# S5's pre-norm applied after its input matmuls, and 256 more transfers issued by GpSimd

## The chip, the cores and the metric

The kernel runs on one core of one Trainium2 chip. The metric is the device time of one execution in microseconds (us): before the change the median of three runs is 2486.29 us (2485.32 to 2488.64). One further execution was taken by the hardware profiler; its own time is 2485.38 us. Engines are named PE (TensorE), DVE (VectorE), ACT (ScalarE), POOL (GpSimd) and SP (SyncE, here only an issuer of DMA transfers); PEld is PE's weight load.

## The reference

A sequence of 512 tokens of 1024 channels goes through two blocks of two layers each, in fp32: a pooling mixer and a gated convolution FFN (ffn0), sliding-window attention and a second such FFN (ffn1); then an S5 mixer and an MLP, an SSD mixer and an MLP. The second block is modulated by a condition vector `c`. What the change touches is this part:

```python
cond = silu(c)
mod = cond @ ada_w[i] + ada_b[i]                  # 1024 x 6144, i = 0, 1
sh1, sc1, g1, sh2, sc2, g2 = split(mod, 6)
h = rmsnorm(x, norm_mix_g[i]) * (1 + sc1) + sh1   # layer 0 of block two: S5
u = h @ s5_w_in
y = s5_recurrence(u, lambda, log_dt, b, c) + d * u
x = x + g1 * (val * sigmoid(gate)),  val, gate = split(gelu(y) @ w_glu + b_glu)
```

## The kernel before

Activations are kept transposed: eight tiles `xT[k]` of 128 channels by 512 tokens. A matrix product in fp32 is made from three matmuls of rounded parts (`mm3`, L218 to L220: high by high, high by low, low by high). A weight chunk `ws` of up to 512 KB is fetched by SP (L190), split by ACT into `wh` (L203) and by DVE into `wl` (L204); three `ws` buffers rotate. Each engine runs a fixed list of instructions in order, and the DMA issues of SP, ACT and POOL stand in such a list too: an issue that waits for a buffer holds what stands behind it in that list.

A layer ends in halves of 256 tokens: its output matmuls (`tail`), the sum of squares `acc` (L294, L295), `Norm.rs` (L303 on PE, L305 on ACT, L306 and L309 on DVE, L312 on PE), which leaves the reciprocal rms on all partitions in PSUM, and then `post_add`, which adds the normed output to `xT` (L434 and L437 on DVE). `post_add` can carry the next layer's pre-norm in its stages. There are two classes of pre-norm. `PreNorm` (L363) waits for the next `Norm.rs`, makes `u = x*gs*rs` (L388), and splits `u + shift` into two parts (L391 on ACT, L392 on DVE) that the matmuls read. `PreScale` (L404) splits `x*gain` inside `post_add` (L418, L419), before the rms is known, and the rms multiplies the matmuls' result. Before the change `PreScale` serves attention and the two FFNs, and `PreNorm` serves S5, SSD and the MLPs.

The modulation (`ada_units`) is a product of a vector and a matrix, made by `vecmat`: twelve blocks of 512 columns, each of eight steps. A step fetches 256 KB as `as` (L483, two buffers) and adds it, scaled, to `aa` on DVE (L486 first, L488 then). At a block's end `aa` is split into three parts by turns of ACT (L496) and DVE (L498), and PE sums over the partitions into a PSUM tile `pn` (L472) that DVE reduces (L475). `aa` has one buffer, and `pn` has one buffer that `vecmat` shares with `Norm.rs`. Generators of such background work are advanced while a layer's matmuls run: S5's tables and matrices beside ffn0 (`d_tab`, `d_k`, `bs`, `cs`, `dd` in the rows), the first modulation and S5's Toeplitz blocks (`tz`, `th`) beside ffn1, the second modulation beside the first MLP. What is left is drained before the next layer.

In S5, `u_out` takes the result of the input matmuls from PSUM with an ACT copy into `usc`, ACT sends it to HBM (`d_u`), and SP fetches it rearranged as `U`. The tables come back from HBM as `vt` (POOL), `rot` and `ct` (SP).

At the start POOL builds four pooling masks (`band`, L830 to L837) that DVE completes (L851) and PE uses (L882).

Of the kernel before, what the change touches and what calls it, by code (L numbers as in the profile page):

```python
# [11 lines left out]
F32 = mybir.dt.float32  # L12
# [9 lines left out]
P = 128  # L22
# [40 lines left out]
def net_kernel(ctx: ExitStack, tc: tile.TileContext, I: dict, out: bass.AP, parts=ALL):  # L63
# [21 lines left out]
    def tt(s="t", dt=F32):  # L85
        return tp.tile([P, S], dt, tag="t", name=nm(s))
# [14 lines left out]
    V.memset(ones, 1.0)  # L101
    one16 = cst.tile([P, 1], BF16, name="one16")
    V.memset(one16, 1.0)
    eps1 = cst.tile([P, 1], F32, name="eps1")
    V.memset(eps1, 1e-6)
    eps2 = cst.tile([P, 1], F32, name="eps2")
    V.memset(eps2, 1e-5)
    mod = cst.tile([P, 96], F32, name="mod")
    cond = cst.tile([P, KD], F32, name="cond")
    cond_set = []  # L110
    recent = {}

# [127 lines left out]
    class Held:  # L240
# [3 lines left out]
        def __init__(self, runs):  # L244
            self.runs, self.ch, self.ap = runs, {}, {}
# [109 lines left out]
    def behind(instructions):  # L355

        with ExitStack() as stack:
            for ins in instructions:
                stack.enter_context(tc.issue_after(ins))
            yield  # L360

    class PreNorm:

        late = False

        def __init__(self, norm, eps, modulate):
            self.norm, self.eps, self.modulate = norm, eps, modulate
            self.h = None
            i, m, gname = modulate
            self.gs = cst.tile([P, KD], F32, tag="gs", bufs=2, name=nm("gs"))  # L370
            c = i * 48 + (m + 1) * 8
            go = voff[gname] + 8 * i
            V.scalar_tensor_tensor(self.gs, mod[:, c:c + 8], 1.0, vec[:, go:go + 8], ALU.add, ALU.mult)

        def parts(self, span):
            return ()
# [27 lines left out]
    class PreScale(PreNorm):  # L404

        late = True

        def __init__(self, norm, eps, gain=None):
            self.norm, self.eps, self.gain = norm, eps, gain
            self.h = [(ht(), ht()) for _ in range(KD)]  # L410
            self.rs = None

        def parts(self, span):

            ts = slice(*span)
            g = [1.0 if self.gain is None else vc(self.gain[0], self.gain[1] + k) for k in range(KD)]
            hi, lo = ([h[i][:, ts] for h in self.h] for i in range(2))
            return (lambda k: A.activation(hi[k], xT[k][:, ts], AF.Copy, scale=g[k]),  # L418
                    lambda k: V.scalar_tensor_tensor(lo[k], xT[k][:, ts], g[k], f(hi[k]), ALU.mult, ALU.subtract))  # L419
# [43 lines left out]

    def vecmat(pool, W, ncb, col, done):

        def total(parts, cb):
            ps = psn.tile([P, 512], F32, tag="n", name=nm("pn"))
            for j in range(3):  # L470
                for q in range(4):
                    T.matmul(ps[:, 4 * q + j:4 * q + j + 1], parts[j][:, q * P:(q + 1) * P], one16,  # L472
                             start=True, stop=True)
            sums = cst.tile([P, 4], F32, tag="asum", bufs=2, name=nm("sums"))
            V.tensor_reduce(sums, ps[:, :16].rearrange("p (q j) -> p q j", q=4)[:, :, :3], AX.X, ALU.add)  # L475
            done(cb, sums)

        due = None
        for cb in range(ncb):
            acc = None  # L480
            for k in range(KD):
                st = pool.tile([P, 512], F32, tag="as", bufs=2, name=nm("as"))
                nc.sync.dma_start(st, W[k * P:(k + 1) * P, cb * 512:(cb + 1) * 512])  # L483
                if k == 0:
                    acc = pool.tile([P, 512], F32, tag="aa", bufs=1, name=nm("aa"))
                    V.tensor_scalar(acc, st, col(k), None, ALU.mult)  # L486
                else:
                    V.scalar_tensor_tensor(acc, st, col(k), acc, ALU.mult, ALU.add)  # L488
                if k % 2:
                    yield  # L490
                if k == 1 and due is not None:
                    total(*due)
            t2 = tt("ab").bitcast(BF16)
            parts = [t2[:, :512], t2[:, 512:], pool.tile([P, 512], BF16, tag="ab", bufs=1, name=nm("ab"))]
            for j in range(3):
                A.activation(parts[j], acc, AF.Copy)  # L496
                if j < 2:
                    V.tensor_tensor(acc, acc, parts[j], ALU.subtract)  # L498
            due = parts, cb
        yield  # L500
        total(*due)

    def ada_units(pool, i):

        if not cond_set:
            cond_set.append(True)
            c0 = voff["c_2"]
            with behind([recent["split"]]):
                A.activation(cond, vec[:, c0:c0 + KD], AF.Silu)
            yield  # L510

        def done(cb, sums):
            c = i * 48 + cb * 4
            bo = voff["ada_b_2"] + c
            V.tensor_tensor(mod[:, c:c + 4], sums, vec[:, bo:bo + 4], ALU.add)

        yield from vecmat(pool, I["ada_w_2"][i], 12, lambda k: cond[:, k:k + 1], done)

    def s5_tables(pool, dr):

# [132 lines left out]
    def s5_phasors(dr, n, far, near):  # L653

        g8 = slice(8 * n, 8 * n + 8)
        wide = lambda t: t.rearrange("p (g a b) -> p g a b", g=8, a=8)
        fr, fi = (t[:, g8].unsqueeze(3).broadcast_to([P, 8, 8, 8]) for t in far)
        nr_, ni_ = (t[:, g8].unsqueeze(2).broadcast_to([P, 8, 8, 8]) for t in near)
        for i, (a, b, c, d, op) in enumerate(((fr, nr_, fi, ni_, ALU.subtract), (fr, ni_, fi, nr_, ALU.add))):
            o, t = tt("ph"), tt("ph")  # L660
            V.tensor_tensor(wide(o), a, b, ALU.mult)
            V.tensor_tensor(wide(t), c, d, ALU.mult)
            V.tensor_tensor(o, o, t, op)
            nc.sync.dma_start(dr["tab"][n][:, 512 * i:512 * i + 512], o)
            yield

    def s5_mats(pool, dr, pr, pi, vr, vi, cr, ci, sg):
        zt = tt("s5z")[:, :P]
        V.memset(zt, 0.0)
        for gb in range(8):  # L670
            nc.sync.dma_start(dr["k"][8 * gb:8 * gb + 8, :, 0].rearrange("g h j -> (g h) j"), zt)
        dg = pool.tile([16, 64], F32, name="s5dg")
        with nc.allow_non_contiguous_dma("4 KB"):
            nc.sync.dma_start(dg, I["s5_d_2"][0].rearrange("(g h) -> h g", h=16))
# [3 lines left out]
        def load(gb):  # L678
            g8 = slice(8 * gb, 8 * gb + 8)
            bs = pool.tile([P, 2, 8, 16], F32, tag="bs", bufs=1, name=nm("bs"))  # L680
            for e, (u, v) in enumerate(((bre, bim), (bim, bre))):
                nc.sync.dma_start(bs[:64, e], u[g8].rearrange("g p h -> p g h"))
                nc.sync.dma_start(bs[64:, e], v[g8].rearrange("g p h -> p g h"))
            cs = pool.tile([P, 2, 2, 64], F32, tag="cs", bufs=1, name=nm("cs"))
            for e, (u, v) in enumerate(((cre, cim), (cim, cre))):
                nc.sync.dma_start(cs[:, e, 0], u[g8].rearrange("g h p -> (g h) p"))
                nc.sync.dma_start(cs[:, e, 1], v[g8].rearrange("g h p -> (g h) p"))
            return bs, cs

        nxt = load(0)  # L690
# [74 lines left out]
    def s5_toeplitz(pool, dr):  # L765

        for n in range(8):
            g8 = slice(8 * n, 8 * n + 8)
            tz = pool.tile([P, 8, P], F32, tag="tz", bufs=2, name=nm("tz"))
            for s in range(8):  # L770
                j = (8 - s) * 16
                nc.sync.dma_start(tz[16 * s:16 * s + 16], dr["kflat"][g8, :, j:j + P].rearrange("g h j -> h g j"))
            yield
            th = pool.tile([P, 8, P], F32, tag="th", bufs=1, name=nm("th"))
            A.activation(th.rearrange("p g (h t) -> p g t h", h=16), tz.rearrange("p g (t h) -> p g t h", t=8), AF.Copy)  # L775
            nc.scalar.dma_start(dr["tab"][n][:, 3072:], th.rearrange("p g j -> p (g j)"))
            yield
# [532 lines left out]
    def s5_layer(dr, pool, pa):  # L1310
# [15 lines left out]
        def ctabs(n):  # L1326
            if n < KD:
                ct[n] = pool.tile([P, 2, 8, P], F32, tag="ct", bufs=2, name=nm("ct"))
                nc.sync.dma_start(ct[n].rearrange("p i g j -> p (i g j)"), dr["tab"][n][:, 2048:])

        def u_out(n, ps, span=FULL):
            if span[0] == 0:
                U[n] = tt("usc")
            usc = U[n]
            cs = slice(span[0] // 8, span[1] // 8)
            a = A.activation(usc.rearrange("p (s c) -> p s c", s=8)[:, :, cs], ps.rearrange("p (c s) -> p s c", s=8),
                             AF.Copy)
# [137 lines left out]
        def tail_(hf, nxt):  # L1475
# [23 lines left out]
            for q in range(2):  # L1499
                glu(6 + q, pp[0][:, 256 * q:256 * q + 256], pp[1][:, 256 * q:256 * q + 256], HALVES[hf])  # L1500

        return Layer(lambda nxt: PreNorm(nxt, eps2, (0, 0, "norm_mix_g_2")), load, head, body_, tail_,
                     lambda span, nxt, pre: None)


# [424 lines left out]
        bgps[0] = psmm  # L1930

    rope_c = {}
    s5_on = "s5" in names
    ada_on = [any(p in names for p in q) for q in (("s5", "mlp0"), ("ssd", "mlp1"))]
    ada_due = [i for i in range(2) if ada_on[i]]
    tables_due, toeplitz_due = s5_on, s5_on
# [103 lines left out]
```

## Time and profile before

| | |
|---|---|
| median of three runs | 2486.29 us (2485.32 to 2488.64) |
| the profiled execution | 2485.38 us, of which the span of its instructions is 2483.7 us |
| PE busy | 2340.7 us, 94% of the span |
| DVE, ACT, POOL busy | 69%, 46%, 14% |
| mean granted PE clock | 0.972 of 2.4 GHz |
| DMA | 311 MB, 125 GB/s on average; SP's queue 278 MB, POOL's 13.6 MB |

The places that the text speaks of, in us from the span's start: the pooling layer up to about 30, ffn0 to 480, attention to 735, ffn1 to 1114 (its tail from 1084), S5's input to about 1180, S5 to 1330.

In the rows, `idle before` in square brackets is how long the engine stood before the instruction, and what released it. The views by window give busy time and number of instructions of each engine, the granted clock and the DMA engines' share. A row of the DMA view ends with the median time from issue to landing.

### The profile page before, as it was taken

What the parts mean: (1) busy time and instruction counts of PE and PEld (TensorE: products, weight loads), DVE (VectorE), ACT (ScalarE), POOL (GpSimd) and SP (SyncE); (2) the same over time, 40 slices, a digit from 0 to 9 for tenths busy, and PEclk for the clock granted to TensorE, in tenths of its full rate; (3) what the DMA queues carried; (4) which work ended last, traced back from release to release, by engine and by line L of the source; (5) the groups of instructions that cost most, each with busy time, mean ns of one, the idle gap of its engine ahead of it and who ended that gap; (6) DMA issues with size and microseconds to landing.
All of it is one profiled execution on the core that took longest, in us unless ns stands there. A gap on an engine that the chain in (4) does not pass through costs nothing.

```text
span 2483.7 us, 33557 instructions
## 1 busy us (share of the span) xinstructions
PE 2340.7 (94%) x12397; PEld 1972.1 (79%) x12397; DVE 1713.8 (69%) x3069; ACT 1142.1 (46%) x2038; POOL 337.9 (14%) x345
## 2 busy tenths in 40 slices
PE   7999999788979999986899999999999999999998
PEld 7877777776778888875878887889878888888888
DVE  6896989678658778786655666666777788633333
ACT  6543535467665444344543433334555554422332
POOL 1001223201200000000110210110143331200110
PEclk9999999889989999997999999999999999999999
DMA  4224443311274555552942455543433332232222
GB/s 122 88 88 140 131 142 103 125 52 51 75 206 134 180 178 165 179 173 68 306 153 77 143 166 191 188 134 92 125 105 99 107 104 80 93 102 94 95 88 72
DMA packets 297780, 311.29 MB, mean 125 GB/s; under 512 B 53569, under 2 KB 251025, under 8 KB 296593
## 3 DMA queue, kind: packets, MB, share of 16 engines
q1 hardware_dynamic: 270033, 278.22, 36.0%
q10 hardware_dynamic: 23680, 17.31, 2.3%
q0 software_dynamic: 3904, 13.63, 1.7%
q8 instruction: 97, 1.59, 0.3%
q14 instruction: 66, 0.54, 0.1%
HBM read 284.92 MB, written 24.18 MB: 124 GB/s over the span
## 4 chain that ended last, share of the span: by engine, by line
PE 74%; DVE 12%; DMA 6%; ACT 4%; issue 3%; SPq 0%; POOL 0%; DVEq 0%; ACTq 0%; POOLq 0%
PE mm L219 22%; PE mm L218 22%; PE mm L220 22%; DMA as<-in_ada_w 3%; DVE wl L204 3%; ACT wh L203 1%; DVE aa L488 1%; PE mm L1642 1%; PE mm L1643 1%; PE mm L1644 1%; PE pb L1712 1%; PE pb L754 1%; DMA tz<-d_k 1%; ACT th L775 1%; DMA d_u<-usc 1%
## 5 line engine op out<-in xcount | busy, mean ns | idle before, releaser
L218 PE MATMUL mm<-h,wh 128*128 128x512 f32 (+1 forms) x1792 | 665.6, 374 | 22.9 <-ACT h L418 7.2
L219 PE MATMUL mm<-h,wh 128*128 128x512 f32 (+1 forms) x1792 | 666.1, 372 | 6.2 <-DVE h L392 3.3
L220 PE MATMUL mm<-h,wl 128*128 128x512 f32 (+1 forms) x1792 | 664.8, 372 | 1.7 <-DVE wl L204 1.7
L203 ACT ACTIVATE wh<-ws 128x1024 fp32r<-128x1024 f32 (+1 forms) x367 | 388.0, 1060 | 563.3 <-PE mm L219 479.6
L204 DVE TENSOR_TENSOR wl<-ws,wh 128x1024 fp32r<-128x1024 f32 (+1 forms) x367 | 466.0, 1272 | 240.7 <-ACT wh L203 234.3
L218 PEld LDWEIGHTS mm<-h,wh 128*128 128x128 f32 x1792 | 346.8, 194 | 81.0 <-issue 8.5
L219 PEld LDWEIGHTS mm<-h,wh 128*128 128x128 f32 x1792 | 347.1, 194 | 63.3 <-DVE h L392 5.4
L220 PEld LDWEIGHTS mm<-h,wl 128*128 128x128 f32 x1792 | 347.3, 194 | 56.3 <-DVE wl L204 2.5
L218 PE MATMUL mm<-hi,wh 128*128 128x512 f32 (+1 forms) x1056 | 369.5, 354 | 9.0 <-ACT wh L203 7.6
L219 PE MATMUL mm<-lo,wh 128*128 128x512 f32 (+1 forms) x1056 | 372.0, 353 | 1.7 <-DVE lo L319 1.7
L220 PE MATMUL mm<-hi,wl 128*128 128x512 f32 (+1 forms) x1056 | 370.8, 353 | 0.8 <-DVE wl L204 0.8
L218 PEld LDWEIGHTS mm<-hi,wh 128*128 128x128 f32 x1056 | 200.6, 190 | 37.3 <-ACT wh L203 8.7
L219 PEld LDWEIGHTS mm<-lo,wh 128*128 128x128 f32 x1056 | 201.4, 191 | 28.5 <-DVE lo L319 2.7
L220 PEld LDWEIGHTS mm<-hi,wl 128*128 128x128 f32 x1056 | 201.2, 191 | 26.8 <-DVE wl L204 1.0
L488 DVE SCALAR_TENSOR_TENSOR aa<-as,cond,aa 128x512 f32<-128x512 f32 x168 | 132.0, 786 | 113.8 <-DMA as<-in_ada_w 112.3
L1266 POOL TENSOR_TENSOR r<-r 128x512 f32<-128x512 f32 x64 | 88.1, 1379 | 671.1 <-ACT r L1262 488.0
L760 POOL TENSOR_TENSOR dd<-ident,s5dg 16x64 f32<-16x64 f32 x16 | 69.4, 4337 | 343.1 <-DVE kt L762 336.1
L319 DVE TENSOR_TENSOR lo<-r,hi 128x512 fp32r<-128x512 f32 x64 | 48.1, 756 | 76.5 <-ACT hi L317 76.4
L1287 DVE SCALAR_TENSOR_TENSOR x<-mm,mod,x 128x512 f32<-128x512 f32 (+1 forms) x76 | 48.9, 662 | 60.6 <-PE mm L220 60.4
L496 ACT ACTIVATE ab<-aa 128x512 bf16<-128x512 f32 x72 | 44.9, 624 | 97.0 <-DVE aa L488 61.7
L317 ACT ACTIVATE hi<-r 128x512 fp32r<-128x512 f32 x64 | 40.4, 631 | 72.3 <-POOL r L1266 72.3
L295 DVE TENSOR_TENSOR acc<-acc,sq 128x256 f32<-128x256 f32 (+1 forms) x148 | 62.0, 432 | 16.4 <-ACT sq L294 11.6
(484 smaller groups left out, 3651.2 us busy)
## 6 DMA issues: line engine op xcount, KB each, us to landing
ws<-in_mlp_w SPq DMA_DIRECT2D x124, 512.0 KB, 4.0
as<-in_ada_w SPq DMA_DIRECT2D x192, 256.0 KB, 3.1
ws<-in_ffn_w_in SPq DMA_DIRECT2D x88, 512.0 KB, 3.8
ws<-in_m_w_in SPq DMA_DIRECT2D x41, 512.0 KB, 3.7
ws<-in_ffn_w_out SPq DMA_DIRECT2D x40, 512.0 KB, 3.5
ws<-in_w_o SPq DMA_DIRECT2D x16, 512.0 KB, 3.4
ct<-d_tab SPq DMA_DIRECT2D x8, 1024.0 KB, 9.5
ws<-in_s_w_glu SPq DMA_DIRECT2D x16, 512.0 KB, 5.8
```

The costliest lines, as they stand in the source:

```text
L203: A.activation(h_, s_, AF.Copy)
L204: V.tensor_tensor(l_, s_, f(h_), ALU.subtract)
L218: T.matmul(ps, wh, xh, start=first, stop=False)
L219: T.matmul(ps, wh, xl, start=False, stop=False)
L220: return T.matmul(ps, wl, xh, start=False, stop=last).ins
L295: V.tensor_tensor(dst, dst, sq[:, a:b], ALU.add)
L319: return hi_, V.tensor_tensor(lo[:, ts], src, f(hi[:, ts]), ALU.subtract)
L488: V.scalar_tensor_tensor(acc, st, col(k), acc, ALU.mult, ALU.add)
L496: A.activation(parts[j], acc, AF.Copy)
L760: G.tensor_tensor(dd, ident[:16, :16].unsqueeze(1).broadcast_to([16, 4, 16]), dg[:, g4].unsqueeze(2).broadcast_to([16, 4, 16]), ALU.mult)
L1266: G.tensor_tensor(r, r, r, ALU.mult)
L1287: V.scalar_tensor_tensor(xT[n][:, ts], ps, md(i, 5, n), xT[n][:, ts], ALU.mult, ALU.add)
```

## The change

S5's pre-norm becomes a `PreScale` with the modulation's gain. The reciprocal rms then multiplies the result of S5's input matmuls in `u_out` (one more DVE instruction on each evacuation), and the shift goes through the matmuls by itself: `s5c = shift @ s5_w_in`, made by two further blocks of `vecmat` behind the first modulation's twelve (16 transfers of 256 KB and 16 DVE steps), and added as ACT's bias.

Besides, these transfers are issued by POOL and no longer by SP: the first modulation's 96 `as` (with the 16 new ones 112), 16 `d_tab<-ph`, 8 `d_k<-s5z`, 32 `bs`, 32 `cs`, 64 `tz` and 8 `ct`. The second modulation stays with SP. The two epsilons move into one tile. Line numbers of the changed kernel are higher by 20 in most places: `as` is issued at L495, steps are L498 and L500, splits L514, the reduce L487, `post_add` L445 and L448.

```diff
     class PreScale:
-        def __init__(self, norm, eps, gain=None):
+        def __init__(self, norm, eps, gain=None, modulate=None):
+            self.norm, self.eps = norm, eps
+            if modulate is not None:
+                gs = modulated(*modulate)
+                self.gain = lambda k: gs[:, k:k + 1]
...
-    def vecmat(pool, W, ncb, col, done):
+    def vecmat(pool, W, ncb, col, done, perm=False, queue=nc.gpsimd):
...
-                nc.sync.dma_start(st, W[k * P:(k + 1) * P, cb * 512:(cb + 1) * 512])
+                queue.dma_start(st, W[k * P:(k + 1) * P, cb * 512:(cb + 1) * 512])
...
-        yield from vecmat(pool, I["ada_w_2"][i], 12, lambda k: cond[:, k:k + 1], done)
+        yield from vecmat(pool, I["ada_w_2"][i], 12, lambda k: cond[:, k:k + 1], done,
+                          queue=nc.sync if i else nc.gpsimd)
+        if i == 0 and s5_on:
+            yield from vecmat(pool, I["s5_w_in_2"][0], 2, lambda k: md(0, 0, k),
+                              lambda cb, sums: V.tensor_copy(s5c[:, 4 * cb:4 * cb + 4], sums), perm=True)
...
-                nc.sync.dma_start(bs[:64, e], u[g8].rearrange("g p h -> p g h"))
+                nc.gpsimd.dma_start(bs[:64, e], u[g8].rearrange("g p h -> p g h"))
...
-                nc.sync.dma_start(ct[n].rearrange("p i g j -> p (i g j)"), dr["tab"][n][:, 2048:])
+                nc.gpsimd.dma_start(ct[n].rearrange("p i g j -> p (i g j)"), dr["tab"][n][:, 2048:])
...
-            a = A.activation(usc.rearrange("p (s c) -> p s c", s=8)[:, :, cs], ps.rearrange("p (c s) -> p s c", s=8),
-                             AF.Copy)
+            t = tt("us")[:, :span[1] - span[0]]
+            V.tensor_tensor(t, ps, S_["pre"].rs[:, slice(*span)], ALU.mult)
+            a = A.activation(usc.rearrange("p (s c) -> p s c", s=8)[:, :, cs], t.rearrange("p (c s) -> p s c", s=8),
+                             AF.Identity, bias=s5c[:, n:n + 1])
...
-        return Layer(lambda nxt: PreNorm(nxt, eps2, (0, 0, "norm_mix_g_2")), load, head, body_, tail_,
+        return Layer(lambda nxt: PreScale(nxt, eps2, modulate=(0, 0, "norm_mix_g_2")), load, head, body_, tail_,
```

The instructions that the rows below name stand in this order on their engines. First DVE at the seam from ffn1 to S5, from the last step of the modulation's twelfth block to the first addition of `post_add` in the kernel before (`f<-f,mm` are ffn1's last sums, `acc` the post-norm's):

```order
L488 SCALAR_TENSOR_TENSOR aa_10079<-as_10115,cond,aa_10079 128x512
L498 TENSOR_TENSOR aa_10079<-aa_10079,ab_10118 128x512
...
L498 TENSOR_TENSOR aa_10079<-aa_10079,ab_10118 128x512
...
L475 TENSOR_REDUCE sums_10138<-pn_10125 128x4
...
L306 RECIPROCAL sr_10359<-sr_10359 128x2
L309 TENSOR_SCALAR dg_10362<-ident,sr_10359 128x128 x2
L979 TENSOR_TENSOR f_8330<-f_8330,mm_10606 128x256
L979 TENSOR_TENSOR f_8346<-f_8346,mm_10606 128x256
L204 TENSOR_TENSOR wl_10771<-ws_10769,wh_10770 128x1024
L434 SCALAR_TENSOR_TENSOR u_10367<-f_8045,vec,pn_10356 128x256
```

The same place of DVE in the changed kernel, from ffn1's last sums to the first addition of `post_add`; `aa_10143` and `aa_10175` are the two blocks of the shift's product, and the twelfth block, with the first steps of `aa_10143`, stands ahead of the piece:

```order
L999 TENSOR_TENSOR f_8346<-f_8346,mm_10675 128x256
...
L500 SCALAR_TENSOR_TENSOR aa_10143<-as_10157,mod,aa_10143 128x512
...
L514 TENSOR_TENSOR aa_10143<-aa_10143,ab_10166 128x4x16x8 x2
L498 TENSOR_SCALAR aa_10175<-as_10173,mod 128x512
...
L500 SCALAR_TENSOR_TENSOR aa_10175<-as_10211,mod,aa_10175 128x512
L514 TENSOR_TENSOR aa_10175<-aa_10175,ab_10214 128x4x16x8
...
L514 TENSOR_TENSOR aa_10175<-aa_10175,ab_10214 128x4x16x8
...
L487 TENSOR_REDUCE sums_10234<-pn_10221 128x4
L537 COPY s5c<-sums_10234 128x4
L308 RECIPROCAL sr_10471<-sr_10471 128x2
L311 TENSOR_SCALAR dg_10474<-ident,sr_10471 128x128 x2
L445 SCALAR_TENSOR_TENSOR u_10479<-f_8045,vec,pn_10468 128x256
```

The last three steps of one block, the whole of another, their splits and their sums now stand between ffn1's last sum and the post-norm's reciprocal.

Second, POOL at the start of the program, before (`band` are the pooling masks, `dd` a product with S5's vector `d`):

```order
L830 AFFINE_SELECT band_164<-band_164 128x128 x2
L832 MEMSET band_178 128x384
L830 AFFINE_SELECT band_178<-band_178 128x128 x3
L837 MEMSET band_178 128x1 x15
L830 AFFINE_SELECT band_178<-band_178 128x128 x2
L760 TENSOR_TENSOR dd_2191<-ident,s5dg 16x64
```

And in the changed kernel, where eight transfers (`bs`, `cs`) stand ahead of the first mask's last parts:

```order
L850 AFFINE_SELECT band_146<-band_146 128x128
L703 DMA bs_1830<-in_s_b_re 64x8x16
L706 DMA cs_1835<-in_s_c_re 128x64
...
L857 MEMSET band_164 128x1 x7
L780 TENSOR_TENSOR dd_2191<-ident,s5dg 16x64
L850 AFFINE_SELECT band_164<-band_164 128x128 x2
L852 MEMSET band_178 128x384
L850 AFFINE_SELECT band_178<-band_178 128x128 x3
L857 MEMSET band_178 128x1 x15
L850 AFFINE_SELECT band_178<-band_178 128x128 x2
```

The product `dd`, which reads the loaded vector `s5dg`, has moved ahead of the last part of the third mask and the whole of the fourth.

## Rows read from the trace of the kernel before

**Rows 1.** The page, busy time of PE and its share.
```profile
PE 2340.7 (94%) x12397; PEld 1972.1 (79%) x12397; DVE 1713.8 (69%) x3069; ACT 1142.1 (46%) x2038; POOL 337.9 (14%) x345
```

**Rows 2.** Windows: us, busy (count) per engine, PEclk, DMA share, GB/s.
```profile
800.00:1050.00 250.00, 249.85 (x1195) 202.22 (x1194) 193.75 (x280) 104.42 (x138) 1.27 (x2) 1.00 0.54 174
...
1120.00:1150.00 30.00, 16.87 (x112) 16.01 (x112) 20.73 (x57) 10.67 (x28) 0.00 (x0) 0.73 0.13 44
```

**Rows 3.** Timeline of PE, the seam: start, us, instruction, idle before.
```profile
1126.67 1.19 PE L303 MATMUL pn<-ones,acc 128*128 128x128 f32 x4 [11.91 <-DVE acc L295]
...
1131.13 0.79 PE L218 MATMUL mm<-h,wh 128*128 128x256 f32 x2 [1.11 <-ACT h L391]
```

**Rows 4.** S5's input sent to HBM: count, ns min/median/max, first and last start.
```profile
L1341 ACTq DMA_DIRECT2D d_u<-usc x8: 366/373/540, 1173.7 to 1199.1; - x8
```

**Rows 5.** Timeline of DVE at the seam.
```profile
1085.63 0.49 DVE L486 TENSOR_SCALAR aa<-as,cond 128x512 f32<-128x512 f32 x1 [1.34 <-ACT ab L496]
...
1096.17 0.75 DVE L488 SCALAR_TENSOR_TENSOR aa<-as,cond,aa 128x512 f32<-128x512 f32 x1 [1.02 <-DMA as<-in_ada_w]
...
1097.62 0.75 DVE L488 SCALAR_TENSOR_TENSOR aa<-as,cond,aa 128x512 f32<-128x512 f32 x1
...
1109.20 0.15 DVE L475 TENSOR_REDUCE sums<-pn 128x4 f32<-128x12 f32 x1
...
1117.31 0.86 DVE L434 SCALAR_TENSOR_TENSOR u<-f,vec,pn 128x256 f32<-128x256 f32 x2
```

**Rows 6.** Timeline of ACT at the seam.
```profile
1098.40 0.63 ACT L496 ACTIVATE ab<-aa 128x512 bf16<-128x512 f32 x1 [12.80 <-DVE aa L488]
...
1104.13 0.62 ACT L496 ACTIVATE ab<-aa 128x512 bf16<-128x512 f32 x1
...
1110.26 0.24 ACT L305 ACTIVATE sr<-pn,eps 128x2 f32<-128x2 f32 x1
```

**Rows 7.** Issue of `as` by SP, ns min/median/max, 740 to 1120.
```profile
L483 SPq DMA_DIRECT2D as<-in_ada_w x94: 327/328/458, 771.9 to 1094.5; - x94
```

**Rows 8.** Issue of `vt` by POOL, the same columns.
```profile
L1321 POOL DMA_DIRECT2D vt<-d_tab x16: 536/536/722, 1002.4 to 1228.1; - x16
```

**Rows 9.** DMA view, 960 to 1060: count, KB, median us to landing.
```profile
as<-in_ada_w SPq DMA_DIRECT2D x33, 256.0 KB, 3.4
...
vt<-d_tab POOLq DMA_DIRECT2D x2, 256.0 KB, 5.2
```

**Rows 10.** DMA view, 1080 to 1120.
```profile
as<-in_ada_w SPq DMA_DIRECT2D x6, 256.0 KB, 2.7
vt<-d_tab POOLq DMA_DIRECT2D x6, 256.0 KB, 6.9
```

**Rows 11.** Timeline of PE at the seam from ffn0 to attention.
```profile
489.00 1.19 PE L312 MATMUL pn<-dg,ones 128*128 128x128 f32 x4 [0.97 <-DVE dg L309]
```

**Rows 12.** Windows, the end of that seam.
```profile
525.00:530.00 5.00, 2.37 (x19) 2.01 (x17) 4.38 (x13) 4.62 (x12) 0.00 (x0) 1.00 0.79 256
```

**Rows 13.** Waits of DVE, 740 to 1120: us, times, longest.
```profile
DVE aa L488 <- DMA as<-in_ada_w: 46.9, 39, 3.0
```

**Rows 14.** Timeline of POOL at the start.
```profile
10.77 0.78 POOL L830 TENSOR_SCALAR_AFFINE_SELECT band<-band 128x128 f32<-128x128 f32 x2
18.42 0.28 POOL L760 TENSOR_TENSOR dd<-ident,s5dg 16x64 f32<-16x64 f32 x1 [6.88 <-DMA s5dg<-in_s_d]
```

**Rows 15.** Timeline of DVE at the start.
```profile
13.94 1.28 DVE L851 TENSOR_TENSOR band<-band,ident 128x128 f32<-128x128 f32 x6
```

**Rows 16.** The page, `dd`: busy, mean ns, idle before.
```profile
L760 POOL TENSOR_TENSOR dd<-ident,s5dg 16x64 f32<-16x64 f32 x16 | 69.4, 4337 | 343.1 <-DVE kt L762 336.1
```

**Rows 17.** Waits of PE, 30 to 480.
```profile
PE mm L218 <- ACT wh L203: 6.1, 3, 3.2
PE mm L218 <- DVE u L939: 6.1, 1, 6.1
```

**Rows 18.** Waits of PE, 640 to 760.
```profile
PE pn L312 <- DVE dg L309: 7.0, 2, 6.1
```

More of the change, by code (lines that the diff above doesn't have):

```diff
@@ L103, in net_kernel @@
     V.memset(one16, 1.0)
-    eps1 = cst.tile([P, 1], F32, name="eps1")
+    eps = cst.tile([P, 2], F32, name="eps")
+    eps1, eps2 = eps[:, 0:1], eps[:, 1:2]
     V.memset(eps1, 1e-6)
-    eps2 = cst.tile([P, 1], F32, name="eps2")
     V.memset(eps2, 1e-5)
@@ L109, in net_kernel @@
     cond = cst.tile([P, KD], F32, name="cond")
+    s5c = cst.tile([P, KD], F32, name="s5c")
+    s5_on = "s5" in parts
     cond_set = []
@@ L360, in behind, with modulated @@
             yield
+    def modulated(i, m, gname):
+        gs = cst.tile([P, KD], F32, tag="gs", bufs=2, name=nm("gs"))
+        c = i * 48 + (m + 1) * 8
+        go = voff[gname] + 8 * i
+        V.scalar_tensor_tensor(gs, mod[:, c:c + 8], 1.0, vec[:, go:go + 8], ALU.add, ALU.mult)
+        return gs
     class PreNorm:
@@ L368, in __init__ @@
             self.h = None
[L369 to L373, printed above, removed]
+            self.gs = modulated(*modulate)
         def parts(self, span):
@@ L406, in net_kernel @@
         late = True
-        def __init__(self, norm, eps, gain=None):
-            self.norm, self.eps, self.gain = norm, eps, gain
+        def __init__(self, norm, eps, gain=None, modulate=None):
[3 more added lines that the diff above has]
+                self.gain = lambda k: gs[:, k:k + 1]
+            else:
+                self.gain = lambda k: 1.0 if gain is None else vc(gain[0], gain[1] + k)
             self.h = [(ht(), ht()) for _ in range(KD)]
@@ L415, in parts @@
             ts = slice(*span)
-            g = [1.0 if self.gain is None else vc(self.gain[0], self.gain[1] + k) for k in range(KD)]
+            g = [self.gain(k) for k in range(KD)]
             hi, lo = ([h[i][:, ts] for h in self.h] for i in range(2))
@@ L494, in vecmat @@
             parts = [t2[:, :512], t2[:, 512:], pool.tile([P, 512], BF16, tag="ab", bufs=1, name=nm("ab"))]
+            pv, av = parts, acc
+            if perm:
+                pv = [p_.rearrange("p (a h g) -> p a h g", h=16, g=8) for p_ in parts]
+                av = acc.rearrange("p (a g h) -> p a h g", g=8, h=16)
             for j in range(3):
-                A.activation(parts[j], acc, AF.Copy)
+                A.activation(pv[j], av, AF.Copy)
                 if j < 2:
-                    V.tensor_tensor(acc, acc, parts[j], ALU.subtract)
+                    V.tensor_tensor(av, av, pv[j], ALU.subtract)
             due = parts, cb
@@ L663, in s5_phasors @@
             V.tensor_tensor(o, o, t, op)
-            nc.sync.dma_start(dr["tab"][n][:, 512 * i:512 * i + 512], o)
+            nc.gpsimd.dma_start(dr["tab"][n][:, 512 * i:512 * i + 512], o)
             yield
@@ L670, in s5_mats @@
         for gb in range(8):
-            nc.sync.dma_start(dr["k"][8 * gb:8 * gb + 8, :, 0].rearrange("g h j -> (g h) j"), zt)
+            nc.gpsimd.dma_start(dr["k"][8 * gb:8 * gb + 8, :, 0].rearrange("g h j -> (g h) j"), zt)
         dg = pool.tile([16, 64], F32, name="s5dg")
@@ L681, in load @@
             for e, (u, v) in enumerate(((bre, bim), (bim, bre))):
-                nc.sync.dma_start(bs[:64, e], u[g8].rearrange("g p h -> p g h"))
-                nc.sync.dma_start(bs[64:, e], v[g8].rearrange("g p h -> p g h"))
+                nc.gpsimd.dma_start(bs[:64, e], u[g8].rearrange("g p h -> p g h"))
+                nc.gpsimd.dma_start(bs[64:, e], v[g8].rearrange("g p h -> p g h"))
             cs = pool.tile([P, 2, 2, 64], F32, tag="cs", bufs=1, name=nm("cs"))
             for e, (u, v) in enumerate(((cre, cim), (cim, cre))):
-                nc.sync.dma_start(cs[:, e, 0], u[g8].rearrange("g h p -> (g h) p"))
-                nc.sync.dma_start(cs[:, e, 1], v[g8].rearrange("g h p -> (g h) p"))
+                nc.gpsimd.dma_start(cs[:, e, 0], u[g8].rearrange("g h p -> (g h) p"))
+                nc.gpsimd.dma_start(cs[:, e, 1], v[g8].rearrange("g h p -> (g h) p"))
             return bs, cs
@@ L771, in s5_toeplitz @@
                 j = (8 - s) * 16
-                nc.sync.dma_start(tz[16 * s:16 * s + 16], dr["kflat"][g8, :, j:j + P].rearrange("g h j -> h g j"))
+                nc.gpsimd.dma_start(tz[16 * s:16 * s + 16], dr["kflat"][g8, :, j:j + P].rearrange("g h j -> h g j"))
             yield
@@ L1932, in net_kernel @@
     rope_c = {}
-    s5_on = "s5" in names
     ada_on = [any(p in names for p in q) for q in (("s5", "mlp0"), ("ssd", "mlp1"))]
```

## The prediction

> **What bounds the kernel now.** I read the page first: PE is busy for 94% of the span [rows 1], so time comes or goes where PE stands or runs slowly, or where an engine that feeds it loses its slack. Then the windows: in ffn1's body PE has 249.85 of 250 us at a clock of 1.00, so whatever the transfers on SP's list do there, it costs nothing today; behind ffn1, from 1120 to 1150, PE has 16.87 of 30 us at 0.73 [rows 2]. Then PE's timeline in that gap: it stands 11.91 us for DVE's sum of squares, and the first of S5's input matmuls comes at 1131.13, behind the rms and the split of h [rows 3]. The first result of that input leaves at 1173.7 [rows 4], 56.4 us after `post_add` begins on DVE at 1117.31 [rows 5]. I call that beginning T0. The late input shortens the way from T0 on, and the two new blocks of `vecmat` stand ahead of T0.
>
> **The seam, ahead of T0.** The order of DVE shows twelfth block, first new block and second new block one after the other, and the sum of the last ahead of the post-norm's reciprocal. PE and ACT cannot change that: `pn` has one buffer, so the post-norm's statistics wait until the last block is summed. Before, only the twelfth block stands there. It starts at 1085.63 [rows 5] and its first split waits until 1098.40 [rows 6], so a block takes 12.8 us; this is the rhythm of two buffers and a landing of 2.7 us [rows 10], with the last step but one still waiting 1.02 us for its transfer [rows 5]. The three ACT parts of the split run from 1098.40 to 1104.75 [rows 6], 6.3 us among ffn1's last work; alone it would be three times 0.63 and two DVE steps about as long, 3.2 us as an estimate. Sum and reduce cost about 1 us. From the post-norm's PE sum to what needs its result I take 4.5 us, which the next norm shows between 1126.67 and 1131.13 [rows 3]. With fetches as fast as today T0 is 1085.6 + 3 x 12.8 + 6.3 + 2 x 3.2 + 1 + 4.5 = 1142.2.
>
> The fetches now come from POOL. An issue takes 0.536 us [rows 8] in place of 0.328 [rows 7], and each block waits for three refills: 9 x 0.21 = 1.9 us. The landing is the unknown. In 960 to 1060 POOL's transfers of the same size took 5.2 us where SP's took 3.4 [rows 9], and at the seam 6.9 against 2.7, though these fell into S5's first loads [rows 10]. After 1120 little is in flight (DMA share 0.13 [rows 2]) and I add nothing there; for the three refills of the block in the crowded stretch I take half of 1.8 each, 2.7 us. T0 becomes about 1146.8, which is 29.5 us later than 1117.3. The lower end is 22 (all splits alone, no surcharge: 1139), the upper 44 (four refills as slow as in [rows 10], 4.2 us more each: 1161).
>
> **The seam, from T0 on.** The trace has the same seam with a `PreScale`: ffn0 to attention. There the post-norm's result is ready at 489.00 + 1.19 = 490.2 [rows 11], and the second half's matmuls end near 527.4 [rows 12], 37.2 us later, clock losses included. S5 needs the new multiplication (0.43 us, half of the 0.86 for two such tiles in [rows 5]), the ACT copy and their handing over before its first transfer; I set 2.7 us for them, an estimate. That is T0 + 39.9 in place of T0 + 56.4, a gain of 16.5 us; its bounds are 12 and 20, since the analog starts with x at another pace. Net of the seam: 29.5 - 16.5 = +13 us (from +5.5 with the lower T0 to +28 with the upper).
>
> **The start.** POOL issues eight transfers ahead of the first mask's last parts, 8 x 0.54 = 4.3 us [rows 8], and `dd` now stands ahead of the fourth mask. In the trace `dd` could not run before `s5dg` landed, at 18.42, while the masks were done at 11.55 [rows 14] and DVE used them at 13.94 [rows 15]. If `s5dg` lands as it does, the fourth mask comes about 3.3 us behind 18.7, at 22. It is the last one that PE needs, so not all of these 8 us count. SP's list is shorter, which may bring `s5dg` forward. I take +4, between 0 (it lands at once) and +11 (it doesn't, and the early `bs` and `cs` stand in the way of x's load).
>
> **ffn1's body.** DVE waited 39 times for `as`, 46.9 us in all [rows 13]. Each of these waits grows by 0.2 us of issue, and by 0 to 1.8 us of landing [rows 9]: 8 to 78 us over the stretch. The cover: DVE idles 56 us of the 250 [rows 2], some 34 of them in these waits, so 22, or 30 over the whole stretch of 345 us, are left until DVE sets PE's pace. That gives 0 at one end and 78 - 30 = +48 at the other. I take +6, near the lower end, since the two POOL transfers behind the 5.2 us were issued one on the other's heels. Behind a DVE step that waits stand the next `wl` and the convolution's steps, and PE waits for both.
>
> **Relief of SP's list.** 256 issues and their buffer waits leave it. Where PE stood for something that may hang on it: 6.1 us for weights and 6.1 for DVE in ffn0 [rows 17], 7.0 us at the entry of ffn1, where `tz` shares the list with the weights [rows 18]. At best this gives 19 us. Against it, POOL now has `dd` (4.3 us on average [rows 16]) ahead of transfers of the tables. I take -4, between -19 and +4. The Trainium skill's page "DMA: Bandwidth & Descriptors" (section "Issuing engines are not separate DMA queues") says that all issuers end on the same 16 engines and that spreading only saves issue time; by it this term is near 0 and the sum 4 us higher. No row shows more than the issue times.
>
> **The rest.** In S5 the `ct` issues move to POOL and stand with its small work, and the new multiplication lies beside PE: 0, between -3 and +3. The epsilons' tile: 0, there is nothing in it but a memset.
>
> Sum: 13 + 4 + 6 - 4 = +19 us. On the profiled execution's 2485.4 that is 2504.4; the median of the runs is 0.9 higher, so 2505.
>
> **Rivals.**
> *SP's list was worth more (faster).* The place is ffn0's end and the entry of ffn1: weights come as soon as their buffer is free, and the 19 us of [rows 17, 18] go. With T0 at its lower end (+5.5), no cost at the start and none in the body, the time is 2486.3 + 5.5 - 19 = 2473. For it: the waits exist and are named. Against: two of the three end on DVE or its diagonal, which have other causes. It decides if the other terms stay under 19 us, which needs T0 before about 1139. Chance 0.2.
>
> *ffn1's body starves (slower by more).* Refills from POOL land as in [rows 9], DVE loses its 30 us of slack, and PE falls behind by up to 48 us: 2505 + 42 = 2547. For it: both rows in which POOL and SP move the same size at the same time show POOL slower. Against: few samples. It decides when the waits for `as` exceed 80 us in this stretch. A cause for it is given by the Trainium skill, "SBUF — State Buffer" (section "Who interferes with whom"): GpSimd cannot write a transfer's descriptors while DVE runs an instruction that takes both ports, a one-input `tensor_scalar` for example. This kernel has one such step a block, of 0.49 us [rows 5], fourteen in all; by the rule they could hold issues for under 7 us. The trace agrees that the other steps don't: `vt` never took over 0.722 us to issue [rows 8]. Chance 0.15.
>
> *Nothing to see.* Lower T0 (+5.5), start and body at +1 each, relief -7: 2487. Chance 0.1.
>
> **How the numbers follow.** The forecast has 0.55. Its own range is 2493 to 2520 (seam from +5.5 to +25, the others near their values). The whole range reaches down into the first rival and up into the second: 2478 to 2535 leaves out about 0.12 below and 0.08 above. A measurement here tells 0.2%, 5 us, from no change. Faster 0.2, the same 0.1, slower 0.55 + 0.15 = 0.7.
>
> **What would show it.** After ffn1's last matmul PE stands for over 20 us, until DVE has summed the second new block, and T0 lies between 1139 and 1160 counted from the same place of ffn1. From T0 the first `d_u` comes within 37 to 44 us. The waits of DVE for `as` in ffn1 rise from 46.9 to between 55 and 90, with PE still near 250 in 800 to 1050. In the pooling layer the last mask's use moves from 13.94 to near 20. I am wrong if T0 moves by less than 16.5 us (the seam then gains), if the refills from POOL land in over 5 us all through ffn1 (far slower), or if the waits of ffn0 and at ffn1's entry vanish (faster).

## The result, and the profile after

The changed kernel takes 2506.86 us (median of 4 runs, 2505.7 to 2507.57), the kernel before 2485.81 (4 runs): a ratio of 1.0084, 95% interval 1.0067 to 1.0102. The forecast was 2505, slower. The total came out as forecast, the terms did not: two large errors cancel. That shows when the two traces are laid against each other at points where both do the same instruction (first or last start, us from the span's start):

| point | before | after | later by | in this stage |
|---|---|---|---|---|
| ffn0's first step (`tg`) | 87.0 | 92.4 | +5.4 | +5.4 start |
| attention's first `kr` | 531.1 | 538.2 | +7.1 | +1.7 ffn0 |
| attention's last `po` | 681.2 | 680.7 | -0.5 | -7.6 attention |
| ffn1's last head step (`tg<-un`) | 761.9 | 749.2 | -12.7 | -12.2 entry of ffn1 |
| ffn1's body, last `lo` | 1083.6 | 1070.4 | -13.2 | -0.5 body |
| ffn1's last sum | 1114.7 | 1102.5 | -12.2 | +1.0 tail |
| first `d_u` | 1173.7 | 1186.9 | +13.2 | +25.4 seam |
| last `py` of S5 | 1260.5 | 1280.5 | +20.0 | +6.8 S5 |
| last step of the last MLP | 2474.2 | 2495.1 | +20.9 | +0.9 the rest |

The seam first. DVE's timeline of the changed kernel, to be read against [rows 5] (columns as there):

```profile
1102.12 0.75 DVE L999 TENSOR_TENSOR f<-f,mm 128x256 f32<-128x256 f32 x2
...
1109.62 0.75 DVE L500 SCALAR_TENSOR_TENSOR aa<-as,mod,aa 128x512 f32<-128x512 f32 x1 [3.41 <-DMA as<-in_s_w_in]
1111.49 1.02 DVE L514 TENSOR_TENSOR aa<-aa,ab 128x512 f32<-128x512 f32 x1 [1.12 <-ACT ab L512]
...
1123.48 0.75 DVE L500 SCALAR_TENSOR_TENSOR aa<-as,mod,aa 128x512 f32<-128x512 f32 x1 [2.12 <-DMA as<-in_s_w_in]
...
1137.26 0.17 DVE L487 TENSOR_REDUCE sums<-pn 128x4 f32<-128x12 f32 x1 [1.19 <-PE pn L484]
...
1140.90 0.87 DVE L445 SCALAR_TENSOR_TENSOR u<-f,vec,pn 128x256 f32<-128x256 f32 x2 [1.19 <-PE pn L314]
```

The last sum of ffn1 ends at 1102.9, and `post_add` begins at 1140.90, 38.0 us later; before, 2.2 us lay between (1115.1 to 1117.31). What has come between is the shift's product (e5 below leaves it out and has 2.2 again). PE's waits from 1100 to 1185, by what ended them (total, times, longest):

```profile
PE pn L484 <- ACT ab L512: 36.8, 6, 14.8
PE pn L314 <- DVE dg L311: 4.9, 3, 3.0
```

Before, PE's longest wait there was for `acc`, 11.91 us [rows 3]; now the long ones are for the split of a background product. In the window from 1102 to 1142 PE has 4 of 40 us and its clock is granted at 0.51, near the lower of its two levels (1.2 of 2.4 GHz):

```profile
1102.00:1142.00 40.00, 4.01 (x32) 2.96 (x32) 19.52 (x36) 9.27 (x16) 8.59 (x16) 0.51 0.31 108
```

The way from `post_add` to the first `d_u` did get shorter, from 56.4 to 46.0 us (the row answers to [rows 4]):

```profile
L1363 ACTq DMA_DIRECT2D d_u<-usc x8: 366/396/1109, 1186.9 to 1212.9; - x8
```

ffn1's body, the answer to [rows 2, 13 and 9], in three views: the window, the waits of DVE from 740 to 1120, and the DMA view from 960 to 1060:

```profile
800.00:1050.00 250.00, 249.99 (x1193) 202.74 (x1193) 194.26 (x285) 102.45 (x135) 43.05 (x80) 1.00 0.54 173
```
```profile
DVE aa L500 <- DMA as<-in_ada_w: 49.6, 35, 3.5
```
```profile
as<-in_ada_w POOLq DMA_DIRECT2D x30, 256.0 KB, 3.0
```

PE is as full as before. POOL's transfers land in 3.0 us where SP's took 3.4, and the waits are 49.6 where they were 46.9.

At the entry of ffn1 the wait of [rows 18] has shrunk from 7.0 to 1.7 us:

```profile
PE pn L314 <- DVE dg L311: 1.7, 1, 1.7
```

The start, POOL and then DVE, against [rows 14, 15]:

```profile
7.05 0.54 POOL L707 DMA_DIRECT2D cs<-in_s_c_re  x1
...
18.68 0.28 POOL L780 TENSOR_TENSOR dd<-ident,s5dg 16x64 f32<-16x64 f32 x1 [5.45 <-DMA s5dg<-in_s_d]
...
21.78 0.66 POOL L850 TENSOR_SCALAR_AFFINE_SELECT band<-band 128x128 f32<-128x128 f32 x2
```
```profile
8.49 0.35 DVE L871 TENSOR_TENSOR band<-band,ident 128x128 f32<-128x128 f32 x1 [7.38 <-POOL band L850]
```

The last mask is ready at 22.4 (before 11.55). But PE's wait for a mask is 0.8 us (before 0.9); what grew is its wait for `xr`, the scaled x, from 1.5 to 4.9 us. The first mask stands at the front of DVE's list, so DVE waits 7.38 us (before 2.20), and its statistics of x come later. In ACT's list the first `rstm`, which needs them, now stands behind all eight squares of x:

```profile
13.68 0.28 ACT L879 ACTIVATE rstm<-ss,eps 128x1 f32<-128x1 f32 x1
```

Before, it came behind three of them, at 6.04.

In S5, `ct` waits on POOL for its buffer, and `dec`, which the recurrence needs, stands behind it:

```profile
1229.11 0.53 POOL L1349 DMA_DIRECT2D ct<-d_tab  x1 [9.81 <-PE py L1405]
1229.63 0.62 POOL L1377 COPY dec<-r 128x512 f32<-128x512 f32 x1
```

### The profile page after: what moved, and what is told of

Same layout as the page of the kernel before. It is cut to its first block, busy times and chain, and to the rows that moved or that the text cites. A ratio compares the mean times of both kernels' runs of the same rounds, so it can differ in the third digit from the quotient of the medians.

```text
span 2504.6 us, 33721 instructions
## 1 busy us (share of the span) xinstructions
PE 2339.9 (93%) x12421; PEld 1971.4 (79%) x12421; DVE 1724.4 (69%) x3089; ACT 1153.7 (46%) x2046; POOL 478.8 (19%) x617
## 4 chain that ended last, share of the span: by engine, by line
PE 67%; DVE 11%; DMA 9%; issue 8%; ACT 4%; POOL 1%; SPq 0%; ACTq 0%; DVEq 0%; POOLq 0%
PE mm L221 20%; PE mm L220 20%; PE mm L222 20%; DMA as<-in_ada_w 5%; DVE wl L206 2%; ACT wh L205 1%; DVE aa L500 1%; PE pb L1734 1%; DMA as<-in_s_w_in 1%; PE mm L1664 1%; PE mm L1665 1%; PE pb L774 1%; DMA ab<-acd 1%; PE mm L1666 1%; DMA tz<-d_k 0%
## 5 line engine op out<-in xcount | busy, mean ns | idle before, releaser
L220 PE MATMUL mm<-h,wh 128*128 128x512 f32 (+1 forms) x1792 | 665.8, 373 | 28.2 <-ACT h L429 11.7
L220 PEld LDWEIGHTS mm<-h,wh 128*128 128x128 f32 x1792 | 345.5, 194 | 86.8 <-ACT h L429 13.4
L1286 POOL TENSOR_TENSOR r<-r 128x512 f32<-128x512 f32 x64 | 86.8, 1360 | 672.2 <-ACT r L1282 440.8
L500 DVE SCALAR_TENSOR_TENSOR aa<-as,cond,aa 128x512 f32<-128x512 f32 x168 | 131.4, 782 | 116.5 <-DMA as<-in_ada_w 115.1
L512 ACT ACTIVATE ab<-aa 128x512 bf16<-128x512 f32 x78 | 51.4, 659 | 127.5 <-DVE aa L500 85.5
L495 POOL DMA_DIRECT2D as<-in_ada_w x96 | 51.8, 539 | 294.2 <-DVE aa L498 121.6
L780 POOL TENSOR_TENSOR dd<-ident,s5dg 16x64 f32<-16x64 f32 x16 | 59.2, 3699 | 86.8 <-DVE kt L782 81.2
```

The source lines that it names most:

```text
L220: T.matmul(ps, wh, xh, start=first, stop=False)
L495: queue.dma_start(st, W[k * P:(k + 1) * P, cb * 512:(cb + 1) * 512])
L512: A.activation(pv[j], av, AF.Copy)
L780: G.tensor_tensor(dd, ident[:16, :16].unsqueeze(1).broadcast_to([16, 4, 16]), dg[:, g4].unsqueeze(2).broadcast_to([16, 4, 16]), ALU.mult)
L1286: G.tensor_tensor(r, r, r, ALU.mult)
```

## The experiments

The kernel before ran beside each lot of them on the same chip, at 2490.8 us in the first and third lot and 2490.1 in the second; the ratios are to that. The prediction's pair had 2485.8, so I read the experiments by their ratios. Their stages are laid against the trace of the kernel before from the prediction's pair: they show where time went, but not to the last few us.

**e1: the transfers without the late input** (the old `PreNorm`, no product for the shift).

```diff
-  PreScale(nxt, eps2, modulate=(0, 0, "norm_mix_g_2"))
+  PreNorm(nxt, eps2, (0, 0, "norm_mix_g_2"))
-  if i == 0 and s5_on:
+  if False:
```

> The transfers are issued by GpSimd as in the changed kernel, but S5 keeps the pre-norm of the kernel before and the two blocks for its shift are gone. If the two halves of the change add up: start +5 us, attention and ffn1's entry -19, S5 up to +7, the seam from ffn1 to S5 as before, in all about 2478 us, and the first d_u some 13 us earlier than the 1173.7 of before. Rival: what was won in attention and at ffn1's entry is an accident of the other order that the new pre-norm brings; then the time is 2486 or more and ffn1 enters at its old time.

Measured 2480.75 us, ratio 0.9957 (0.9944 to 0.9970). Start +5.7 us, ffn0 +3.0, attention -5.1, entry -11.7, body -1.2, tail -1.4, seam -0.7 (first `d_u` at 1162.3), S5 +6.7. The first theory holds: the gains in attention and at the entry, the cost of the start and that of S5 belong to the moved transfers. Attention and entry give 16.8 us where 19 were expected.

**e2: the late input without the moved transfers** (all `nc.gpsimd` of the change back to `nc.sync`).

> The late input with its two blocks, all transfers issued by SyncE as before. If the seam's loss is the wait for the two blocks: T0 lies about 34 us behind ffn1's last sum (before: 2), the first d_u comes 20 to 26 us later than before, in all 2503 to 2512 us, with start, attention and ffn1's entry as before. Rival: the slow refills of GpSimd made the loss; then the refills by SyncE bring T0 back to within 25 us of ffn1's last sum and the time to about 2495. Second rival: the gain in attention comes with the late input; then about 2490.

Measured 2520.61 us, ratio 1.0109 (1.0092 to 1.0126). That is 27 us by the ratio (30 by the medians), more than the 17 to 26 expected; the first `d_u` is 29.7 us later, and ffn1's tail alone is 4.4 us longer. The last sum and `post_add`:

```profile
1123.01 0.75 DVE L999 TENSOR_TENSOR f<-f,mm 128x256 f32<-128x256 f32 x2
...
1157.75 0.87 DVE L445 SCALAR_TENSOR_TENSOR u<-f,vec,pn 128x256 f32<-128x256 f32 x2 [1.18 <-PE pn L314]
```

T0 is 34.0 us behind the last sum with SP issuing, 38.0 with POOL. So the queue is not the cause of the loss, the blocks are. Start and attention are as before, the entry is 2.4 us earlier (759.5 against 761.9), which excludes the second rival. Halves and whole: -0.43% and +1.09% make +0.66%, against +0.84% measured for the change, each known to 0.13 to 0.18: they add up within their intervals.

**e3: the blocks summed within ffn1's body** (`ffn_layer(1, ..., rate=5)` in place of 3).

> The changed kernel with ffn1's background work advanced by five steps for each pair of hidden blocks (before three), so that all fourteen blocks of the products are summed within ffn1's body, ahead of the tail. If the two blocks in front of the post-norm are the loss: T0 follows ffn1's last sum within 4 us, the first d_u is 30 to 40 us earlier than the changed kernel's 1186.9, in all 2467 to 2478 us. Rival: DVE has no room for it in the body; PE then loses in 740 to 1080 what the seam gains, and the time stays at 2490 to 2507.

Measured 2503.76 us, ratio 1.0053 (1.0036 to 1.0070). T0 now comes with the last sums, but the last sum is at 1144.6 and not 1102.5: the first `d_u` is where it was (1186.7). The rival's outcome holds, but not for its reason: DVE is not full (37.5 of 50 us from 900 to 950). The first row is from PE's waits from 740 to 1150, the second from its timeline:

```profile
PE pn L484 <- ACT ab L512: 20.9, 8, 11.9
```
```profile
918.54 0.27 PE L484 MATMUL pn<-one,ab 128*128 128x1 bf16 x4 [11.91 <-ACT ab L512]
```

The sums stand in PE's list too, and when a block is late, PE stands at four matmuls of one column.

**e4: only `tz` by GpSimd**, in the kernel before (one line, `nc.sync` to `nc.gpsimd`), and **e8**, the same kernel executed once more for its trace (2479.85 us).

> The kernel before with only the 64 transfers tz issued by GpSimd. If ffn1's entry was held by weights that stood behind tz in SyncE's list: PE's 7.0 us wait at the entry goes, the entry is 10 to 14 us earlier, in all 2472 to 2477 us, and 6 us more if attention's gain has the same cause. Rival: it takes the transfers of the modulation as well; then the entry is within 4 us of before and the time 2482 to 2487.

> The kernel before with only tz issued by GpSimd, once more for its trace. If tz alone frees the weights: PE's 7.0 us wait at ffn1's entry is under 2, ffn1's last head step (tg<-un) starts at 748 to 752 where before it started at 761.9, and attention up to its last po is as before (681). Rival: the entry is still late by over 6 us and the gain of its time lies elsewhere.

e4 measured 2480.94 us, ratio 0.9957 (0.9944 to 0.9971): 10 us less, which on the prediction's 2485.8 is 2475 and inside the range expected. In e8 ffn1's last head step is at 751.8 (before 761.9) and attention ends at 680.9 as before. PE's wait at the entry is at the bound given:

```profile
PE pn L312 <- DVE dg L309: 2.0, 2, 1.1
```

So tz alone frees the entry. It does not give attention's 5 to 8 us. But the reason expected, weights behind `tz` in SP's list, is not what the traces show: from 680 to 750 no weight split of ACT in the kernel before waited for its transfer. PE's wait of 6.1 us [rows 18] ended on the diagonal, the diagonal waited for ACT's `sr`, and `sr` stood in ACT's list behind the last copy `th`. That copy waited for the transfer of the copy before it (`d_tab<-th`; `th` has one buffer). ACT in the kernel before:

```profile
733.74 2.03 ACT L775 ACTIVATE th<-tz 128x1024 f32<-128x1024 f32 x1 [5.50 <-DMA d_tab<-th]
...
736.18 0.26 ACT L305 ACTIVATE sr<-pn,eps 128x2 f32<-128x2 f32 x1 [0.40 <-ACT th L775]
```

In e8 ACT's list has come out in another order: five copies stand ahead of the same `sr` and three behind it, and `sr` waits for PE alone:

```profile
724.80 0.26 ACT L305 ACTIVATE sr<-pn,eps 128x2 f32<-128x2 f32 x1 [0.40 <-PE mm L220]
...
729.56 2.10 ACT L775 ACTIVATE th<-tz 128x1024 f32<-128x1024 f32 x1
```

How much of the 10 us is this order and how much the landing of `tz` itself was not separated.

**e5: no product for the shift** (`s5c` set to zero, the two blocks left out; the shift's part of S5's input is missing).

> The changed kernel without the two blocks of the shift's product: s5c is set to zero, so the shift's part of S5's input is left out. It prices the late input without what stands in front of it. If the loss at the seam is the wait for the two blocks alone: T0 within 4 us of ffn1's last sum, the first d_u 10 to 16 us earlier than in the kernel with the moved transfers and the old pre-norm, in all 2464 to 2472 us against its 2481. Rival: the late input saves nothing in itself, since its evacuation waits for the second half's rms; then 2478 to 2484.

Measured 2469.93 us, ratio 0.9921 (0.9908 to 0.9935). T0 is 2.2 us behind the last sum, the first `d_u` is 11.1 us earlier than in e1 and 35.7 earlier than in the changed kernel:

```profile
L1364 ACTq DMA_DIRECT2D d_u<-usc x8: 366/402/1843, 1151.2 to 1177.3; - x8
```

The late input itself gains 11 us at the first `d_u`, its shift costs 36. The rival, no gain, falls.

**e6: start and `ct` back with SyncE**, the old pre-norm.

```diff
-  nc.gpsimd.dma_start(bs[:64, e], ...)
+  (nc.sync if gb == 0 else nc.gpsimd).dma_start(bs[:64, e], ...)
-  nc.gpsimd.dma_start(ct[n]..., ...)
+  nc.sync.dma_start(ct[n]..., ...)
```

> The old pre-norm; the transfers by GpSimd except those of the start (first bs and cs, the zeroes d_k) and ct, which go back to SyncE. If the early bs and cs with the masks behind them cost the start, and ct's place behind GpSimd's work cost S5: first ffn0 step at 88 and not 93, S5 6 us shorter, in all 2468 to 2472 us. Rival for the start: dd's place ahead of the fourth mask is what counts, then the start stays 3 to 5 us late. Rival for S5: its 6 us have another cause, then 2474 to 2477.

Measured 2473.70 us, ratio 0.9936 (0.9923 to 0.9948). The time is between the two rivals' ranges, the stages are clear: ffn0 begins at 89.0 (e1: 92.7), and from first `d_u` to last `py` S5 takes 88.2 us (e1: 93.5, before: 86.8). That `ct`'s place cost S5 its time is shown. At the start it is shown that the transfers in POOL's list cost it; but with them gone `dd` stands behind the fourth mask again (at 19.90, the masks done at 11.77), so the rival for the start is not excluded by this run. Against it stand PE's waits in the changed kernel, 0.8 us for a mask and 4.9 for `xr`.

**e7: e3 with four buffers for `as`** (and one for `tz`, to make room).

> The kernel with five steps per pair of hidden blocks, now with four buffers for as and one (not two) for tz. There PE stood for the sums (pn<-one,ab) while DVE waited for as. If the two buffers of as are the cause: DVE's waits for as fall from 62 us to under 15, PE's stand at the sums from 21 us to under 6, ffn1's body ends near 1075 and the time is 2468 to 2480 us. Rival: the sums' place in PE's list ahead of the split is the cause, whatever the buffers; then the body still ends after 1095 and the time is 2490 to 2505.

Measured 2470.79 us, ratio 0.9929 (0.9914 to 0.9944). The body ends at 1073.7, and PE has no wait at the sums over 0.8 us. DVE's waits for `as` from 740 to 1150, in e3 and in e7:

```profile
DVE aa L500 <- DMA as<-in_ada_w: 62.3, 40, 5.0
```
```profile
DVE aa L500 <- DMA as<-in_ada_w: 6.6, 7, 2.2
```

From 62 to 6.6 us: the two buffers were the cause, and DVE has room for all fourteen blocks.

**e10: four buffers alone** (and one for `tz`, as in e7), the blocks at their place ahead of the post-norm.

> The changed kernel with four buffers for as and one for tz alone; the two blocks still stand ahead of the post-norm. If the price of the two blocks was mostly the refills that each step waits for: T0 lies 14 to 22 us behind ffn1's last sum (changed kernel 38), in all 2484 to 2493 us. Rival: the splits and sums by turns of ACT, DVE and PE are the larger part; then T0 stays over 28 us behind and the time is 2496 to 2505.

Measured 2485.30 us, ratio 0.9976 (0.9967 to 0.9985). T0 lies at 1120.01, 21.8 us behind the last sum and so at the upper end of the first theory. Of the 38 us the refills held 16; the splits by turns, the steps themselves and the sums hold the rest.

**e9: all of it**: late input, four buffers, pace of five, start and `ct` with SyncE.

> The late input with four buffers for as, one for tz and five steps of background work per pair, and the start's transfers and ct back with SyncE. If the costs found add up: 2470.8 less 4 us at the start and 3 to 5 in S5, in all 2461 to 2465 us. Rival: ct by SyncE stands behind the weights that the late input now wants earlier; then S5 gains nothing and the time is 2466 to 2470.

Measured 2462.22 us, ratio 0.9882 (0.9868 to 0.9895), faster than both kernels: by the ratios 29 us less than before and 50 less than the changed one. ffn0 begins at 88.0 and S5 takes 88 us, so the rival falls. The body stays full:

```profile
800.00:1050.00 250.00, 250.00 (x1222) 200.35 (x1221) 214.07 (x317) 113.44 (x150) 50.57 (x94) 1.00 0.59 188
```

## Why the prediction was right, and where it was not

*The seam, ahead of T0*: the mechanism is the forecast one (one `pn`, three blocks in a row, the reduce ahead of the reciprocal). The size was +29.5 and is +35.8 (38.0 less 2.2). The term mis-sized is the split: I set 3.2 us for one alone, and the first of them ran from 1110.40 to 1115.74, 5.3 us, because the new blocks are split through a permuted view. ACT's part takes 1.06 us, where [rows 6] have 0.63, and DVE's 1.02, where the twelfth block's takes 0.69. The second ran from 1129.73 to 1136.90, 7.2 us, with the post-norm's squares in between. Together that is 6.1 us more than the two times 3.2, and so nearly all of the miss:

```profile
1110.40 1.06 ACT L512 ACTIVATE ab<-aa 128x512 bf16<-128x512 f32 x1 [10.42 <-DVE aa L500]
1112.54 1.06 ACT L512 ACTIVATE ab<-aa 128x512 bf16<-128x512 f32 x1 [1.08 <-DVE aa L514]
1114.68 1.06 ACT L512 ACTIVATE ab<-aa 128x512 bf16<-128x512 f32 x1 [1.08 <-DVE aa L514]
1129.73 1.06 ACT L512 ACTIVATE ab<-aa 128x512 bf16<-128x512 f32 x1 [13.99 <-DVE aa L500]
1130.69 0.40 ACT L293 ACTIVATE acc<-f 128x256 f32<-128x256 f32 x1
```

The last line shows that the one `pn` is not the only hold. The post-norm's squares, which need no `pn`, stand behind the second block's split in ACT's list. They are summed at 1136.07, and the reduce that frees `pn` ends at 1137.43: in this order the shared tile itself holds the post-norm for little over 1 us. No run gave `pn` a second buffer, so what that would do to the order is not shown.

*From T0 on*: forecast a gain of 16.5, measured 10.4. The matmuls end where the analog put them: the second half's at 1178, T0 + 37. But what followed took 9 us and not the 2.7 that I set. The analog had shown a part of it: its matmuls end at 526.69 (the busy time in [rows 12] is not unbroken, so 527.4 was read 0.7 too late), and then PE stood 2.00 us for the second half's rms, which the prediction left out:

```profile
526.41 0.28 PE L220 MATMUL mm<-h,wl 128*128 128x256 f32 x1
528.69 0.68 PE L312 MATMUL pn<-dg,ones 128*128 128x128 f32 x4 [2.00 <-ACT wh L194]
```

In the changed kernel DVE's list has three weight splits of 1.9 us ahead of the second half's rms, and a fourth behind the first multiplication; PE waits for that rms (3.0 us at L314 in the waits above):

```profile
1176.61 3.77 DVE L206 TENSOR_TENSOR wl<-ws,wh 128x1024 fp32r<-128x1024 f32 x2 [0.23 <-ACT wh L205]
1180.29 0.16 DVE L308 RECIPROCAL sr<-sr 128x2 f32<-128x2 f32 x1
...
1180.88 0.42 DVE L1357 TENSOR_TENSOR us<-mm,rsx 128x256 f32<-128x256 f32 x1
```

So the seam is +25 where I had +13, inside the bounds given (+5.5 to +28). e5 and e1 price its two parts: 36 for the blocks, -11 for the late input.

*The start*: +4 forecast, +5.4 measured. The fourth mask is ready at 22.4 as worked out (22), but PE hardly waited for it. The time went another way, by the first mask and the statistics of x behind it, which was not in the working; that the two come out alike is luck.

*ffn1's body*: +6 forecast, -0.5 measured. The step that failed is the landing: I took a share of the 5.2 against 3.4 of [rows 9], which were two transfers issued back to back. Spread out, POOL's land in 3.0 us. So the rival that starved the body finds nothing to bite on. For the rule that the prediction quoted beside it from the Trainium skill, "SBUF — State Buffer" ("Who interferes with whom"), the trace shows no stall of that kind: with DVE 78% busy (800 to 1050) the longest of 96 issues is 0.590 us:

```profile
L495 POOL DMA_DIRECT2D as<-in_ada_w x96: 536/538/590, 665.2 to 1081.2; - x96
```

*Relief of SP's list*: -4 forecast, about -20 measured (attention -7.6, entry -12.2). This is the largest miss. [rows 18] had the entry's wait, and I discounted it because it ended on DVE. The step that failed is that I followed the wait no further: the diagonal waited for ACT's `sr`, and `sr` stood behind a `th` that waited for its buffer (e8). The rule quoted from "DMA: Bandwidth & Descriptors" (the Trainium skill, "Issuing engines are not separate DMA queues") would have made this term near 0. Here it does not decide: the moved `tz` was worth 10 us in e4, and the wait that went with it was one of ACT's list and not issue time. Attention's share comes in e1, e3, e5, e6, e7, e9 and e10 and not in e2 and e8. PE's order in attention is that of the kernel before in e2 and e8 and another one in the changed kernel, in e1 and in e6; its clock from 620 to 650 is 1.00 in the changed kernel and in e1, in place of 0.89. Which of the moved transfers brings that stays open: not tz alone (e8), and not the start's or `ct` (e6 has them back with SP and keeps the gain).

*The rest*: S5 was set at 0, within 3, and is +6.8, 5.3 of it the `ct` issue in front of `dec` (e6). ffn0, ffn1's tail and the last layers add 3.6 that no term had.

The first rival (SP's list worth 19) was right about its term and lost because the seam cost 25 and not 5.5. Of the signs that the prediction named, T0 came where it said (38.0 us behind ffn1's last sum, which is 1153 on the scale of before), but the first `d_u` came 46.0 us behind T0 and not 37 to 44, DVE's waits for `as` were 49.6 us and not 55 to 90, and the wait at ffn1's entry, whose end was to mean "faster", did shrink, to 1.7 us. The large errors are -16 and -6.5 on one side, +12.4 and +6.8 on the other, and that they cancel is luck; the order of DVE, which decided the sign, was read rightly.

## What to carry to other kernels

A background product that is cheap in work can be dear in place: ask which buffer it shares with the next step of the main line (here one PSUM tile), where it stands in the lists of the engines that this step needs, and whether it ends before that step. Moving an issue moves its wait, and with it the order of other engines' lists: ahead of the masks and of `dec` it cost 12 us of the 17 that it gained elsewhere (e1). So follow a wait to the instruction that was late first, and not only to the engine that it ends on. Two buffers for a stream whose steps take 0.75 us and whose transfers take 3 us to land left DVE waiting 35 times in ffn1 (49.6 us); with the blocks at the same place, the third and fourth buffer were worth 27 us (e10 against the changed kernel, by the ratios), the choice of the issuer 11 (e1).

## What the runs showed that was not expected

256 KB from GpSimd landed in 3.0 us (median, 960 to 1060), no longer than the 3.4 that SyncE's took in the same stretch of the kernel before (the trace has the landing of 9 of those 33), though its issue takes 0.538 us against 0.328. The permuted view makes a part of the split 1.06 us in place of 0.63 on ACT and 1.02 in place of 0.69 on DVE. And PE stood 11.91 us at four one-column matmuls of 0.27 us in e3.
